# Moving weight splits behind later ScalarE copies, and alternating accumulator banks, in a block-matrix up-projection

## The chip, the cores and the metric

The kernel runs on one core of one Trainium2 chip. The metric is device time in microseconds (us); a run's time is that of its one core. The kernel before was timed three times: 1277.96, 1278.49 and 1284.9 us, median 1278.49.

## What is computed

A two-layer decoder trunk on 512 tokens of width 1024, float32. Each layer has a sequence mixer (mLSTM and forgetting attention in layer 0, Mamba-2 and pooling in layer 1), a layer norm, a gated convolutional FFN and a second layer norm:

```
def conv_ffn(x, w_up, conv_w, conv_b, w_down):
    h = causal_dwconv(x @ w_up, conv_w, conv_b)      # width 3 along the sequence
    val, gate = jnp.split(h, 2, axis=-1)
    return (jax.nn.silu(gate) * val) @ w_down        # D_FF = 2816

x = layer_norm(ALPHA * x + y, ln1_g[layer], ln1_b[layer])
f = conv_ffn(x, ffn_w_up[layer], ffn_conv_w[layer], ffn_conv_b[layer], ffn_w_down[layer])
x = layer_norm(ALPHA * x + f, ln2_g[layer], ln2_b[layer])
```

The change touches only `x @ w_up`, once per layer.

## The kernel before

Every float32 operand is cut into two parts, hi and lo, and a matrix product is three products of parts: hi by hi, lo by hi, hi by lo. The cut of a weight tile (`split`, L284) is a copy to hi on ScalarE (ACT, L285), then a subtraction that gives lo on VectorE (DVE, L286). Five hi and five lo buffers serve all weight tiles.

**Direct tiles.** The up-projection has 22 gate tiles and 22 value tiles, each 128 features wide. A pair (one gate, one value) can be computed directly: `mtile` loads a weight tile, splits it and issues 24 matmuls of 512 columns (L238). `gated` (L996) then does the convolution: per tile an ACT activation (L990) and two DVE operations (L992), then a Silu (L998) and a DVE product (L1000).

**Rounds.** Eight of the 22 pairs are computed directly. The other fourteen are taken two pairs at a time in `up_quarters` (L1022): seven rounds per layer (j = 3, 6, ..., 21), each with a Strassen-Winograd scheme on 2 by 2 blocks, which needs seven block products in place of eight. A round has four weight blocks W11, W12, W21, W22 (512 KB each). Sums of weight blocks are made by DMA: a transfer issued on GpSimd (POOL) that adds a block from HBM onto a tile already in SBUF. Sums of the activations (E, S2, S3, S4) are made once per layer, in round 1. In the order of the code, a round does:

- load W11 into c and W12 into d (L1087, L1089; four buffers, so that loads run up to two rounds ahead), W21 and W22 into two "raw" buffers (L1090, L1091). The loads are issued on SP.
- L1092: d += W22. This is called d's sum below.
- Product 1: split c, x = c times A11; ACT copies it to g (L1099).
- L1100: c += W12, the first sum.
- Product 2: split W21, o = W21 times A12; DVE adds it to g (L1105).
- Product 3: split c, y = c times E; ACT copies it to v (L1110).
- L1111: c += W22, the second sum.
- The direct pair j + 1 (two tiles), except in round 7.
- Product 4: split c, x += c times S2; ACT copies to v (L1117).
- L1118: c += W21, the third sum.
- Product 5: split d, x += d times S3; DVE (L1122). Product 6: split W22, y += W22 times S4; DVE (L1126).
- Product 7: split c, x += c times A22; ACT copies to g (L1130), first for pair half i = 0, then for i = 1; then `gated` of both pairs.

Each product is done for the two halves i = 0 and 1, each 12 matmuls of 256 columns (L1069). The two halves' x tiles accumulate through the round in two banks of PSUM with the tag "S" (L1095), of which there are two in all; "tp" and "av" are two further banks, used elsewhere in the kernel for transposes and the output projections. The remaining four banks ("mm") hold o, y and the direct tiles. So the x of a round takes the banks that the x of the round before held until its L1130 copies.

**Order.** The program is written in the order above, but a scheduler at compile time orders each engine's instructions by when, by its own estimate of times, their inputs are ready. An instruction may stand on its engine ahead of ones that come earlier in the code. The emitted order is fixed; at run time each engine takes its instructions one after another, and an instruction that waits holds up those behind it. `tc.issue_after(ins)` adds an edge for the scheduler: instructions traced in its block that run on the engine of `ins` are placed behind `ins`; it puts no wait into the program.

Of the kernel before, what the change touches and what calls it, by code (L numbers as in the profile page):

```python
# [16 lines left out]
NJ = DFF // P  # L17
# [89 lines left out]
def trunk(ctx: ExitStack, tc: tile.TileContext, W, x, xT, cols, rows, poolw, consts, out):  # L107
# [15 lines left out]
    def nm(s):  # L123
        uid[0] += 1
        return f"{s}_{uid[0]}"

    def ps(tag="mm"):
        return pp.tile([P, 512], F32, tag=tag, name=nm(tag), bufs={"mm": 4, "S": 2, "tp": 1, "av": 1}[tag])
# [39 lines left out]
    def c1(i):  # L168
        return col[:, i:i + 1]
# [114 lines left out]
    def split(src, hi, lo, lo_eng=None):  # L284
        A.activation(hi, src, AF.Copy)  # L285
        (lo_eng or V).tensor_tensor(lo, src, r32(hi), ALU.subtract)  # L286
# [696 lines left out]

    def ffn(pool, layer, up, dn, last):
        cw, cb = C_FW[layer], C_FB[layer]
        act = [pool.tile([P, 2, S], F32, tag="a", name=nm("a"), bufs=NJ // 2) for _ in range(NJ // 2)]

        def conv(j, o):
            c = tmp()
            A.activation(c, o, AF.Identity, bias=c1(cb + j), scale=c1(cw + 2 * 2 * NJ + j))  # L990
            for d in range(1, 3):
                V.scalar_tensor_tensor(c[:, d:], o[:, :S - d], c1(cw + (2 - d) * 2 * NJ + j), c[:, d:],  # L992
                                       ALU.mult, ALU.add)
            return c

        def gated(j, g, v):  # L996
            gt = conv(NJ + j, g())
            A.activation(gt, gt, AF.Silu)  # L998
            vl = conv(j, v())
            V.tensor_tensor(act[j // 2][:, j % 2, :], vl, gt, ALU.mult)  # L1000

        with tc.tile_pool(name=f"up{layer}", bufs=1, side="left") as work:
            up_quarters(work, up, gated)
        after_ln[:] = [None, 0]
        for t in range(NT):
            xk[t] = rp.tile([P, D], F32, tag="x", name=nm("xk"), bufs=4)
            nc.sync.dma_start(xk[t], away[t])
        with tc.tile_pool(name=f"dn{layer}", bufs=1, side="left") as work:
            early = [0, 1]

            def two(b):
                if early:
                    early.pop()
                    hi, lo = (wp.tile([P, D], F32R, tag=g, name=nm("s"), bufs=5).rearrange("p (a b) -> p a b", a=2)
                              for g in ("hi", "lo"))
                else:
                    hi, lo = (work.tile([P, 2, S], F32R, tag="s", name=nm("s"), bufs=11) for _ in range(2))
                split(act[b], hi, lo, G)
                return [(hi[:, i, :], lo[:, i, :]) for i in range(2)]
            proj_ln(two, range(NJ), dn, 2 * layer + 1, None if last else OD)  # L1020

    def up_quarters(pool, up, gated):  # L1022

        L, R = slice(0, 256), slice(256, 512)

        def quarter(h, t):
            return [xcur[2 * part + h][:, :, t] for part in range(2)]

        A11, A12, A21, A22 = quarter(0, L), quarter(1, L), quarter(0, R), quarter(1, R)

        def wide(tag, dt=F32):
            return pool.tile([P, 4, 256], dt, tag=tag, name=nm(tag), bufs=1)

        def pair():
            return [pool.tile([P, 4, 256], F32R, tag="o", name=nm("o"), bufs=6) for _ in range(2)]

        def total(eng, d, terms):

            eng.tensor_tensor(d, r32(terms[0][1][0]), r32(terms[1][1][0]), ALU.add if terms[1][0] > 0 else ALU.subtract)  # L1041
            for sign, a in ((terms[0][0], terms[0][1][1]), (terms[1][0], terms[1][1][1])):
                eng.tensor_tensor(d, d, r32(a), ALU.add if sign > 0 else ALU.subtract)  # L1043

        def more(eng, d, s, a, op):
            eng.tensor_tensor(d, s, r32(a[0]), op)
            eng.tensor_tensor(d, d, r32(a[1]), op)

        gated(0, lambda: mtile(up), lambda: mtile(up + 1))
        e, s2 = wide("e"), wide("t")  # L1050
        total(V, e, [(1, A22), (-1, A21)])
        E, S2, S3 = pair(), pair(), pair()
        split(e, *E)
        more(V, s2, e, A11, ALU.add)
        A.activation(S2[0], s2, AF.Copy, scale=-1.0)
        V.scalar_tensor_tensor(S2[1], s2, -1.0, r32(S2[0]), ALU.mult, ALU.subtract)
        gated(1, lambda: mtile(up + 2), lambda: mtile(up + 3))

        def wsplit(p):
            hi = wp.tile([P, D], F32R, tag="hi", name=nm("hi"), bufs=5)  # L1060
            lo = wp.tile([P, D], F32R, tag="lo", name=nm("lo"), bufs=5)
            split(p, hi, lo)
            return hi, lo

        def mul(o, w, half, a, start=True):
            n = 0
            for ww, part in ((w[0], 0), (w[1], 0), (w[0], 1)):
                for k in range(4):
                    T.matmul(o[:, L], ww[:, half * 512 + k * P:half * 512 + (k + 1) * P], a[part][:, k, :],  # L1069
                             start=start and n == 0, stop=n == 11, skip_group_check=not start)  # L1070
                    n += 1

        for j in range(3, NJ, 3):
            js = (j - 1, j)
            W11, W12, W21, W22 = (W[up + 2 * (j - 1) + i] for i in range(4))
            if j == 3:
                for i in range(4):
                    sl = slice(i, i + 1)
                    total(G, e[:, sl], [(1, [a[:, sl] for a in A11]), (-1, [a[:, sl] for a in A21])])
                    split(e[:, sl], *(a[:, sl] for a in S3))  # L1080
                S4 = wide("e", F32R), wide("f", F32R)
                for i in range(4):
                    sl = slice(i, i + 1)
                    more(G, s2[:, sl], s2[:, sl], [a[:, sl] for a in A12], ALU.subtract)
                    split(s2[:, sl], *(a[:, sl] for a in S4))
            c, d = (rp.tile([P, D], F32, tag="x", name=nm("c"), bufs=4) for _ in range(2))
            nc.sync.dma_start(c, W11)  # L1087
            e21, e22 = wraw(), wraw()
            nc.sync.dma_start(d, W12)  # L1089
            nc.sync.dma_start(e21, W21)  # L1090
            nc.sync.dma_start(e22, W22)  # L1091
            nc.gpsimd.dma_start(d, W22, accum_op=ALU.add)  # L1092
            g = [pool.tile([P, S], F32, tag="g", name=nm("g"), bufs=2) for _ in js]
            v = [pool.tile([P, S], F32, tag="v", name=nm("v"), bufs=2) for _ in js]
            x = [ps("S") for _ in js]  # L1095
            w = wsplit(c)
            for i in range(2):
                mul(x[i], w, i, A11)
                A.activation(g[i][:, L], x[i][:, L], AF.Copy)  # L1099
            nc.gpsimd.dma_start(c, W12, accum_op=ALU.add)  # L1100
            w = wsplit(e21)
            for i in range(2):
                o = ps()
                mul(o, w, i, A12)
                V.tensor_tensor(g[i][:, L], g[i][:, L], o[:, L], ALU.add)  # L1105
            w = wsplit(c)
            y = [ps() for _ in js]
            for i in range(2):
                mul(y[i], w, i, E)
                A.activation(v[i][:, R], y[i][:, L], AF.Copy, scale=-1.0)  # L1110
            nc.gpsimd.dma_start(c, W22, accum_op=ALU.add)  # L1111
            if j + 1 < NJ:
                gated(j + 1, lambda: mtile(up + 2 * j + 2), lambda: mtile(up + 2 * j + 3))
            w = wsplit(c)
            for i in range(2):
                mul(x[i], w, i, S2, False)
                A.activation(v[i][:, L], x[i][:, L], AF.Copy)  # L1117
            nc.gpsimd.dma_start(c, W21, accum_op=ALU.add)  # L1118
            w = wsplit(d)
            for i in range(2):  # L1120
                mul(x[i], w, i, S3, False)
                V.tensor_tensor(v[i][:, R], v[i][:, R], x[i][:, L], ALU.subtract)  # L1122
            w = wsplit(e22)
            for i in range(2):
                mul(y[i], w, i, S4, False)
                V.scalar_tensor_tensor(v[i][:, L], v[i][:, L], -1.0, y[i][:, L], ALU.mult, ALU.subtract)  # L1126
            w = wsplit(c)
            for i in range(2):
                mul(x[i], w, i, A22, False)
                A.activation(g[i][:, R], x[i][:, L], AF.Copy)  # L1130
                gated(js[i], lambda: g[i], lambda: v[i])

    with tc.tile_pool(name="ev", bufs=1, side="left") as pool:
# [120 lines left out]
```

## Time and profile before

| | |
|---|---|
| times of three runs | 1277.96, 1278.49, 1284.9 us |
| the profiled execution: time, span | 1282.55 us, 1280.5 us |
| TensorE matmul (PE) busy | 1169.7 us, 91% |
| VectorE (DVE) busy | 838.7 us, 65% |
| ScalarE (ACT) busy | 563.0 us, 44% |
| GpSimd (POOL) busy | 335.0 us, 26% |
| TensorE's mean granted clock, share of full | 0.955 |

The span runs from the first to the last instruction of the profiled execution; some 2 us lie around it. The rounds of layer 0 lie between about 266 and 557 us of the span, those of layer 1 between about 856 and 1145 us. The busy share of PE counts a matmul at half clock as busy for twice as long.

### The profile page before, as it was taken

How to read it: one execution, taken by the hardware profiler on the slowest of the kernel's cores; microseconds unless marked ns; L12 is line 12 of the kernel's file. 1: busy time of each engine (PE TensorE's matmuls, PEld its weight loads, DVE VectorE, ACT ScalarE, POOL GpSimd, SP SyncE). 2: the span in 40 equal slices, each digit the busy share in tenths (PEclk: the TensorE clock that was granted, in tenths of full speed). 3: DMA queues.
4: the chain of work that ended last, by engine and by line, in shares of the span. 5: the costliest groups of instructions: out<-in, count | busy, mean ns of one | idle time of the engine just before them, and what ended most of it. 6: DMA issues, size and time to landing. Idle time of an engine off the chain costs nothing. (4 is left out here: it accounts for less than half of the span.)

```text
span 1280.5 us, 16455 instructions
## 1 busy us (share of the span) xinstructions
PE 1169.7 (91%) x6320; PEld 1000.5 (78%) x6320; DVE 838.7 (65%) x1254; ACT 563.0 (44%) x889; POOL 335.0 (26%) x330
## 2 busy tenths in 40 slices
PE   8999999997789888989999999998888888998997
PEld 6777788876789778978887766777777778987886
DVE  5978555696556656674548978687665655675545
ACT  5446533134444544463324466324354543455330
POOL 1223222125010001047422066025100101027442
PEclk9999999998899888989999999998888889999998
DMA  8322421264656465463323142345545465544211
GB/s 289 110 98 88 159 84 66 99 201 102 141 134 159 119 148 118 115 194 100 99 66 119 51 137 98 116 137 138 139 129 148 110 154 132 149 115 158 93 46 66
DMA packets 47950, 157.70 MB, mean 123 GB/s; under 512 B 5352, under 2 KB 5992, under 8 KB 47872
## 3 DMA queue, kind: packets, MB, share of 16 engines
q1 hardware_dynamic: 39648, 126.77, 29.6%
q0 software_dynamic: 8224, 29.89, 13.4%
q8 instruction: 49, 0.80, 0.2%
q14 instruction: 29, 0.24, 0.1%
HBM read 150.30 MB, written 6.34 MB: 122 GB/s over the span
## 5 line engine op out<-in xcount | busy, mean ns | idle before, releaser
L286 DVE TENSOR_TENSOR lo<-raw,hi 128x1024 fp32r<-128x1024 f32 (+1 forms) x173 | 239.6, 1390 | 128.1 <-ACT hi L285 127.5
L238 PE MATMUL mm<-xT,hi 128*128 128x512 f32 (+1 forms) x1088 | 281.6, 400 | 2.0 <-ACT xT L285 2.0
L285 ACT ACTIVATE hi<-raw 128x1024 fp32r<-128x1024 f32 (+1 forms) x175 | 172.2, 989 | 168.2 <-PE mm L336 102.4
L238 PEld LDWEIGHTS mm<-xT,hi 128*128 128x128 f32 x1088 | 202.4, 191 | 45.6 <-issue 4.4
L286 DVE TENSOR_TENSOR lo<-c,hi 128x1024 fp32r<-128x1024 f32 x70 | 84.3, 1220 | 123.1 <-ACT hi L285 123.1
L285 ACT ACTIVATE hi<-c 128x1024 fp32r<-128x1024 f32 x70 | 73.7, 1056 | 183.6 <-DMA c<-in_W 175.1
L286 POOL TENSOR_TENSOR s<-a,s 128x1024 fp32r<-128x1024 f32 x44 | 119.0, 2719 | 108.0 <-PE mm L336 54.5
L238 PE MATMUL mm<-xT,lo 128*128 128x512 f32 (+1 forms) x544 | 139.8, 393 | 0.0
L1069 PE MATMUL S<-xT,hi 128*128 128x256 f32 x448 | 85.1, 333 | 57.2 <-ACT g L1130 52.3
L336 PE MATMUL mm<-hi,s 128*128 128x512 f32 (+1 forms) x396 | 120.9, 385 | 6.6 <-POOL s L286 5.9
L1069 PEld LDWEIGHTS S<-xT,hi 128*128 128x128 f32 x448 | 75.3, 240 | 60.1 <-ACT g L1130 54.4
L238 PEld LDWEIGHTS mm<-xT,lo 128*128 128x128 f32 x544 | 101.7, 190 | 21.7 <-issue 1.9
L336 PEld LDWEIGHTS mm<-hi,s 128*128 128x128 f32 x396 | 74.9, 192 | 21.9 <-POOL s L286 6.9
L992 DVE SCALAR_TENSOR_TENSOR tmp<-mm,col,tmp 128x511 f32<-128x511 f32 (+1 forms) x64 | 47.3, 747 | 51.0 <-ACT tmp L990 50.0
L336 PE MATMUL mm<-lo,s 128*128 128x512 f32 (+1 forms) x198 | 75.8, 383 | 0.0
L1069 PE MATMUL S<-o,hi 128*128 128x256 f32 x448 | 65.3, 283 | 1.2 <-ACT v L1117 1.2
L1069 PEld LDWEIGHTS S<-o,hi 128*128 128x128 f32 x448 | 59.5, 191 | 2.3 <-ACT v L1117 1.4
L336 PE MATMUL S<-hi,s 128*128 128x512 f32 x176 | 56.9, 390 | 0.0
L990 ACT ACTIVATE tmp<-mm,col 128x512 f32<-128x512 f32 x32 | 24.6, 776 | 67.7 <-PE mm L238 58.8
L314 POOL TENSOR_SCALAR small<-small 128x1 f32<-128x1 f32 (+2 forms) x25 | 13.7, 548 | 154.8 <-DVE small L413 93.4
L1069 PE MATMUL mm<-o,hi 128*128 128x256 f32 x224 | 36.0, 294 | 17.2 <-DVE tmp L992 14.6
L1092 POOL DMA_DIRECT2D c<-in_W x14 | 12.3, 880 | 150.2 <-DMA c<-in_W 62.6
(286 smaller groups left out, 2241.8 us busy)
## 6 DMA issues: line engine op xcount, KB each, us to landing
raw<-in_W SPq DMA_DIRECT2D x162, 512.0 KB, 3.7
c<-in_W POOLq DMA_DIRECT2D x56, 512.0 KB, 7.1
c<-in_W SPq DMA_DIRECT2D x28, 512.0 KB, 3.9
bc<-dr SPq DMA_DIRECT2D x20, 256.0 KB, 4.1
tmp<-in_rows SPq DMA_DIRECT2D x16, 256.0 KB, 3.9
away<-xk SPq DMA_DIRECT2D x8, 512.0 KB, 2.6
xk<-away SPq DMA_DIRECT2D x8, 512.0 KB, 6.7
raw<-in_W SPq DMA_DIRECT2D x8, 256.0 KB, 5.7
```

The source lines that it names most:

```text
L238: T.matmul(o[:, :cols_], w[:, k * P:(k + 1) * P], xs_(xcur, part, k)[:, :cols_], start=n == 0, stop=n == 3 * NK - 1)
L285: A.activation(hi, src, AF.Copy)
L286: (lo_eng or V).tensor_tensor(lo, src, r32(hi), ALU.subtract)
L314: G.tensor_scalar(dst, var, EPS, None, ALU.add)
L336: T.matmul(o[:, c], a[:, t * P:(t + 1) * P], ww[:, kk * 512 + c.start:kk * 512 + c.stop], start=first and kk == 0 and n == 0, stop=fin and ...
L990: A.activation(c, o, AF.Identity, bias=c1(cb + j), scale=c1(cw + 2 * 2 * NJ + j))
L992: V.scalar_tensor_tensor(c[:, d:], o[:, :S - d], c1(cw + (2 - d) * 2 * NJ + j), c[:, d:], ALU.mult, ALU.add)
L1069: T.matmul(o[:, L], ww[:, half * 512 + k * P:half * 512 + (k + 1) * P], a[part][:, k, :], start=start and n == 0, stop=n == 11, skip_group ...
L1092: nc.gpsimd.dma_start(d, W22, accum_op=ALU.add)
```

## The change

Three edits, all in the rounds.

1. **Order on ACT.** `wsplit` gets a second argument. The hi copy of the first sum (product 3) is placed behind the L1130 copy of half i = 0 of the round before (`box["quarter"]`; in round 1 behind the last L1099 copy of the same round). The hi copy of the second sum (product 4) is placed behind the last L1110 copy of product 3. The hi copy of the third sum (product 7) is placed behind the convolution's first activation (L990) of the value tile of the direct pair; in round 7, which has none, behind the last L1110 copy. The subtractions on DVE get no edge.
2. **Banks.** The x tiles of a round use "tp" and "av" in odd rounds and the two "S" banks in even ones.
3. **d's sum** is written after the first sum in the code, behind product 1's copies, and no longer right behind the loads.

```diff
     def ffn(pool, layer, up, dn, last):
+        box = {}
         def conv(j, o):
             c = tmp()
-            A.activation(c, o, AF.Identity, bias=c1(cb + j), scale=c1(cw + 2 * 2 * NJ + j))
+            box["conv"] = A.activation(c, o, AF.Identity, bias=c1(cb + j), scale=c1(cw + 2 * 2 * NJ + j)).ins
...
-        def wsplit(p):
+        def wsplit(p, after=None):
             hi = wp.tile([P, D], F32R, tag="hi", name=nm("hi"), bufs=5)
             lo = wp.tile([P, D], F32R, tag="lo", name=nm("lo"), bufs=5)
-            split(p, hi, lo)
+            if after is None:
+                split(p, hi, lo)
+            else:
+                with tc.issue_after(after):
+                    split(p, hi, lo)
             return hi, lo
...
-            nc.gpsimd.dma_start(d, W22, accum_op=ALU.add)
-            x = [ps("S") for _ in js]
+            x = [ps(b) for b in (("S", "S"), ("tp", "av"))[j // 3 % 2]]
             w = wsplit(c)
             for i in range(2):
                 mul(x[i], w, i, A11)
-                A.activation(g[i][:, L], x[i][:, L], AF.Copy)
+                got = A.activation(g[i][:, L], x[i][:, L], AF.Copy).ins
             nc.gpsimd.dma_start(c, W12, accum_op=ALU.add)
+            nc.gpsimd.dma_start(d, W22, accum_op=ALU.add)
...
-            w = wsplit(c)
+            w = wsplit(c, box.get("quarter", got))
             y = [ps() for _ in js]
             for i in range(2):
                 mul(y[i], w, i, E)
-                A.activation(v[i][:, R], y[i][:, L], AF.Copy, scale=-1.0)
+                got = A.activation(v[i][:, R], y[i][:, L], AF.Copy, scale=-1.0).ins
             nc.gpsimd.dma_start(c, W22, accum_op=ALU.add)
             if j + 1 < NJ:
                 gated(j + 1, lambda: mtile(up + 2 * j + 2), lambda: mtile(up + 2 * j + 3))
-            w = wsplit(c)
+                mid = box["conv"]
+            else:
+                mid = got
+            w = wsplit(c, got)
...
-            w = wsplit(c)
+            w = wsplit(c, mid)
             for i in range(2):
                 mul(x[i], w, i, A22, False)
-                A.activation(g[i][:, R], x[i][:, L], AF.Copy)
+                got = A.activation(g[i][:, R], x[i][:, L], AF.Copy).ins
+                if i == 0:
+                    box["quarter"] = got
                 gated(js[i], lambda: g[i], lambda: v[i])
```

## Rows read from the trace of the kernel before

**Rows 1.** Waits: engine, tile, line, releaser: us in total, times, longest.
```profile
PE S L1069 <- ACT g L1130: 52.3, 10, 6.2
```

**Rows 2.** The chain that ended last, 915 to 1000 us: start, us, what.
```profile
916.10 1.24 DVE lo L286
917.35 3.62 DMA c<-in_W
...
921.55 0.52 POOL c L1092
922.07 9.18 DMA c<-in_W
...
933.66 5.49 PE S L1069 x24
```

**Rows 3.** Timeline of PE, 340 to 420 us: start, us, instruction, [idle before].
```profile
371.55 0.64 PE L1069 MATMUL mm<-e,hi 128*128 128x256 f32 x4
...
376.83 0.64 PE L1069 MATMUL S<-xT,hi 128*128 128x256 f32 x4
381.77 1.22 PE L1069 MATMUL S<-xT,hi 128*128 128x256 f32 x4 [4.30 <-ACT g L1130]
```

**Rows 4.** Timeline of ACT, 340 to 420 us.
```profile
363.51 1.06 ACT L285 ACTIVATE hi<-c 128x1024 fp32r<-128x1024 f32 x1 [2.17 <-DMA c<-in_W]
...
366.00 0.78 ACT L990 ACTIVATE tmp<-mm,col 128x512 f32<-128x512 f32 x1 [0.91 <-PE mm L238]
366.68 1.05 ACT L285 ACTIVATE hi<-c 128x1024 fp32r<-128x1024 f32 x1
...
369.15 1.05 ACT L285 ACTIVATE hi<-raw 128x1024 fp32r<-128x1024 f32 x1
379.45 1.06 ACT L285 ACTIVATE hi<-c 128x1024 fp32r<-128x1024 f32 x1 [9.24 <-DMA c<-in_W]
```

**Rows 5.** Windows over product 1 of ten rounds: us, PE, PEld busy, PEclk, DMA, GB/s.
```profile
381.77:387.00 5.23, 5.23 (x26) 5.23 (x26) 0.53 0.68 116
...
sum 51.54, PE 51.52 PEld 51.53; mean PE 5.15 PEld 5.15
```

**Rows 6.** The chain that ended last, into round 7 of layer 1.
```profile
1115.47 2.88 PE mm L1069 x24
1118.35 5.76 PE S L1069 x48
```

**Rows 7.** Issue to landing of L1100, then of L1118: us min/median/max.
```profile
DMA to landing us min/median/max: 5.1/9.2/11.1
...
DMA to landing us min/median/max: 7.1/7.4/8.5
```

**Rows 8.** Timelines of POOL and ACT into round 7 of layer 0.
```profile
523.71 0.86 POOL L1100 DMA_DIRECT2D c<-in_W  x1 [12.81 <-DVE lo L286]
...
529.10 1.06 ACT L285 ACTIVATE hi<-c 128x1024 fp32r<-128x1024 f32 x1 [4.97 <-DMA c<-in_W]
```

**Rows 9.** Timeline of DVE, 340 to 420 us.
```profile
380.53 1.22 DVE L286 TENSOR_TENSOR lo<-c,hi 128x1024 fp32r<-128x1024 f32 x1 [6.92 <-ACT hi L285]
...
390.96 1.22 DVE L286 TENSOR_TENSOR lo<-raw,hi 128x1024 fp32r<-128x1024 f32 x1
```

**Rows 10.** Round 1: timelines of PE and ACT, layer 1, then layer 0.
```profile
901.61 1.20 PE L1069 MATMUL mm<-o,hi 128*128 128x256 f32 x4 [8.81 <-DVE tmp L992]
...
900.54 0.36 ACT L1099 ACTIVATE g<-S 128x256 f32<-128x256 f32 x1
...
309.89 0.55 PE L1069 MATMUL mm<-o,hi 128*128 128x256 f32 x1 [5.80 <-DVE tmp L992]
...
294.94 1.06 ACT L285 ACTIVATE hi<-c 128x1024 fp32r<-128x1024 f32 x1 [9.49 <-DMA c<-in_W]
```

**Rows 11.** Round 7 of layer 0: timeline of ACT.
```profile
536.94 2.01 ACT L285 ACTIVATE hi<-c 128x1024 fp32r<-128x1024 f32 x2 [2.27 <-DMA c<-in_W]
...
540.59 0.65 ACT L1110 ACTIVATE v<-mm 128x256 f32<-128x256 f32 x2
```

More of the change, by code (lines that the diff above doesn't have):

```diff
@@ L1002, in ffn @@
         with tc.tile_pool(name=f"up{layer}", bufs=1, side="left") as work:
-            up_quarters(work, up, gated)
+            up_quarters(work, up, gated, box)
         after_ln[:] = [None, 0]
@@ L1020, in ffn, with up_quarters @@
             proj_ln(two, range(NJ), dn, 2 * layer + 1, None if last else OD)
-    def up_quarters(pool, up, gated):
+    def up_quarters(pool, up, gated, box):
         L, R = slice(0, 256), slice(256, 512)
```

## The prediction, made before the changed kernel ran

> **What bounds the kernel now.** I read the page first: PE is busy 91% of the span, every other engine much less, so time is won only where PE waits or runs at a lower clock. The view of waits names the largest wait of PE that repeats: ten times, 52.3 us in total, the first matmul of a round waits for an L1130 copy [rows 1]. Ten is five a layer, the starts of rounds 2 to 6. The timelines show one of them, from round 2 to round 3. PE ends product 7 at 376.83 + 0.64 = 377.47 us and stands 4.30 us [rows 3]. ACT meanwhile stands 9.24 us before the hi copy of the next round's first sum, which the scheduler put ahead of the L1130 copies; it starts when the DMA lands, at 379.45 [rows 4]. So x's bank comes free late because ACT waits for a sum that PE needs only two products later.
>
> The chain of waits says why the sum is late: the third sum's lo, then d's load (3.62 us), d's sum issued on POOL, and the first sum behind it, 9.18 us, with the bank wait at its end [rows 2]. Here d is that of two rounds on, c that of the next.
>
> The wait costs twice. Product 1 after it takes 5.23 us at a granted clock of 0.53, near the lower of the two levels, 1.2 of 2.4 GHz, after 4.30 us without a matmul; ten of them take 51.54 us [rows 5]. A product at full clock takes 2.88 us [rows 6]. Round 7 starts without a gap, products 7 and 1 together in 5.76 us [rows 6]: that is what a round's start is without this wait.
>
> **The change, part by part.** The sum is made against the profiled execution, 1282.55 us with a span of 1280.5; that is 4.06 us above the median of the runs, 1278.49, and I carry the difference over to the median.
>
> *Banks (edit 2).* The x of a round takes banks that the round before doesn't use, so product 1 no longer waits for L1130. The wait goes: -52.3 us [rows 1]. With PE fed, product 1 stays at the upper clock: ten times 5.15 - 2.88 = 2.27 us, -22.7 us [rows 5, 6]. Together -75.0 us. What is late next? Not product 1's operands: W11's hi copy runs at 366.68, ten microseconds ahead [rows 4]. Next is what DVE and ACT must do before the following products, which is the next term.
>
> *First sum behind L1130 of half 0 (edits 1 and 3).* The hi copy now stands behind one L1130 copy but still ahead of the other and of the two pairs' convolutions. When does the sum land? The third sum's hi copy, now at 363.51, must go behind the L990 of 366.00 [rows 4]. That takes ACT's place after 366.68, so W11's hi copy moves on by up to 1.06 us, and the sum's issue to about 371.2. d's load follows the third sum's lo (about 369) and takes 3.62 us [rows 2], so d's sum is ready near 372.6 and should be issued after the first sum, whichever stands first in the code. Free of d's sum, the first sum took 529.10 - 523.71 = 5.4 us in round 7 [rows 8]; behind it the median is 9.2 [rows 7]. I take 7.4 us, the third sum's median [rows 7], since the new place has two ordinary loads beside it as the third sum has. So it lands at 378.6, 1.1 us after product 7's end.
>
> From there DVE decides. Between lo of the first sum (380.53) and the end of lo of the first direct tile (392.18) lie 11.65 us [rows 9], nearly all packed DVE work (convolutions, products). Some 2.1 of it (a lo, an L1126, short waits for PE) can now run before, which leaves 9.5. So that lo is ready at 378.6 + 1.1 + 9.5 = 389.2; PE wants it after products 1 to 3 and eight hi matmuls of 512 columns (a matmul of 256 columns is 2.88 / 24 = 0.12 us, so these are 1.9), at 377.47 + 3 x 2.88 + 1.9 = 388.0. Stall 1.2 us, ten times: +12. Ends: none if the sum lands after 5.4 us, 3.0 each (+30) if after 9.2.
>
> *Third sum behind the direct tile (edit 1).* Its split now falls into the stretch in which W22 for product 6 is split. That hi copy runs at 369.15 and its product starts at 371.55 [rows 3, 4]; pushed by 1.06 us to end at 371.3, its lo (1.2 us) would be ready at 372.5, 0.5 us after the four hi matmuls are through. By priority in the code the scheduler may keep it in place. I take 0.3 us in twelve rounds (1 to 6, two layers): +3.6, between 0 and 12.7. The second sum's hi, behind L1110, is not used before the direct tiles are done (48 matmuls of 512 columns, some 11 us at 0.24 each); they hide it.
>
> *Round 7 (edit 1).* Here no direct tiles stand between, and the chain of sums is PE's limit. The second sum's hi copy ran at 536.94, ahead of L1110 at 540.59 [rows 11]; now it comes behind it, at 540.59 + 0.65 = 541.2 at the latest, 4.3 us later. But product 4 can't start before product 3 is done, which is about when L1110 runs, so most of the 4.3 us was spent waiting anyway, and PE loses only what of hi and lo the old order had already done by then. I take 0.7 us. Twice: +1.4, between 0 and 2 x 4.3.
>
> *Round 1 (edit 1).* The first sum waits behind the last L1099. In layer 1 that copy runs at 900.54, while product 3's first half was already done; its second half stood until 901.61 for a convolution on DVE [rows 10]. The first half now joins it: +1.44 us. In layer 0 the hi copy blocked ACT for 9.49 us, and the same product waited 5.80 us [rows 10]; ACT gets that time back, but DVE's queue still leads there. I take 1.44 twice, +2.9; ends -5.8 and +2 x 2.9.
>
> Sum: -75.0 + 12 + 3.6 + 1.4 + 2.9 = -55.1. The profiled execution would take 1227.4, the median run **1223 us**.
>
> ScalarE's order deserves a second look, since the wait is moved and not removed. The row shows an ACT that stands 9.24 us before one copy while L1130's matmuls had ended [rows 4]. The Trainium skill (PSUM — Partial Sum Buffer, section Engine vs sequencer instructions) says that the queues of ScalarE, VectorE and GpSimd are strictly first in, first out; the trace agrees. By that rule the waiting copy, one place further on, still holds the second L1130 copy and both convolutions, which is the second rival below; free of it, the sum would stand at -67.1 rather than -55.1.
>
> The row on landing is 7.4 us for the third sum against 5.4 for the unaccompanied first [rows 7, 8]. The Trainium skill (DMA: Bandwidth & Descriptors, section Issuing engines are not separate DMA queues) says that transfers from all issuing engines run on the same 16 engines and interleave, so taking d's sum from in front leaves the loads on SP beside it. With 5.4 the sum would be -67, with 7.4 it is -55.
>
> **The rivals.**
>
> *A: the first sum still lands late.* If W11's lo slips, or the scheduler keeps d's sum in front with its data there in time, the landing is 9.2 us after an issue at 371.2, at 380.4, and the stall 3.0 us each; with the other added terms at twice my value the gain is 75.0 - 30 - 16 = 29. For it: POOL takes requests in order and the edit leaves each round's d far ahead. Against: d's load now ends later. Time 1250, within 1233 to 1263.
>
> *B, the other side: d's sum stays ahead and waits for its load.* POOL then stands until d's load lands, 369 + 3.62 = 372.6; the first sum is issued at 373.2 and lands 9.2 later at 382.4, 4.9 us after product 7. ACT can't do L1130 of half 1 or the convolutions before; the direct tile's lo comes at 393.0, 5.0 us late, and product 1's low clock is paid there instead (2.3 us, rows 5). That is 7.3 of the 7.5 us that a round start gives back; with the other terms at their upper middle (+16) the time is 1278.5 - 2 + 16 = 1292. It decides when the sum lands more than about 4 us after product 7. For it: the chain of waits runs through just these steps today [rows 2]. Against: by the scheduler's own clock the first sum should be ready first.
>
> *C: the scheduler arranges it otherwise*, so that the banks are free and another wait of the same length (a direct tile's weight, a weight buffer) takes its place: within 6 us of 1278.
>
> **How the numbers follow.** Forecast 0.68, A 0.17, C 0.07, B 0.08. The forecast's own range is 1204 (all terms but -75 at nothing) to 1238. For 8 in 10 I reach into A: **1204 to 1254**. What this kernel's timing can tell from no change is about 0.5%, 6.4 us. Faster: forecast and A and a little of C, 0.87; same: most of C, 0.05; slower: B, 0.08.
>
> **What would show it.** Right: no wait for L1130 at PE; product 1 of rounds 2 to 6 at 2.9 us and a clock of 1.0; rounds 2 to 6 of 31 to 33 us each (7 x 2.88 for products and 11 for the direct pair is 31.1); the first sum issued before d's and landing within 8 us. Wrong on the third term: PE stalls of over 2 us before the first direct tile, with lo on DVE as releaser. Wrong on round 1 or 7: product 3 of round 1 or product 4 of round 7 over 3 us later than said. The prediction as a whole is wrong if a gap of over 3 us still recurs in rounds 2 to 6.

## The result, and the profile after

The changed kernel takes 1207.3 us (median of four runs, one of them disturbed, at 2359 us, and left out of the ratio) against 1280.5 for the kernel before on the same chip: a ratio of 0.9411, 95% interval 0.9363 to 0.9459. The prediction said 1223 with a range of 1204 to 1254. The profiled execution took 1201.96 us, 80.6 less than that of before. Line numbers below are those of the changed kernel: product matmuls L1075, the copies L1104, L1116, L1126 and L1139 (before: L1099, L1110, L1117, L1130), first sum L1105, d's sum L1106, second sum L1117, third sum L1127; each experiment shifts them by a line or a few.

The page: span, busy shares, granted clock in 40 slices.

```profile
span 1199.5 us, 16425 instructions
PE 1141.1 (95%) x6320; PEld 973.1 (81%) x6320; DVE 832.0 (69%) x1254; ACT 562.9 (47%) x889; POOL 339.2 (28%) x330
PEclk9999999999899999999999999999899999999999
```

The waits of PE, to be held against [rows 1]: no wait for L1139 is left. The largest is one in round 1 of each layer.

```profile
PE mm L1075 <- ACT hi L285: 19.0, 2, 10.2
PE mm L336 <- POOL s L286: 7.6, 4, 3.2
PE S L261 <- ACT xT L285: 5.3, 2, 4.2
```

The timeline of PE over the start of round 3, to be held against [rows 3]: product 7 ends and product 1 follows without a gap, now in "tp" and "av".

```profile
365.52 0.64 PE L1075 MATMUL S<-xT,hi 128*128 128x256 f32 x4
366.00 0.64 PE L1075 MATMUL tp<-xT,hi 128*128 128x256 f32 x4
```

The windows over product 1 of rounds 2 to 6 in both layers, to be held against [rows 5] (columns also DVE, ACT and POOL busy): ten times 2.88 us at a granted clock of 1.00, which is 2.4 GHz, where it was 5.15 us at about half of that.

```profile
366.00:368.88 2.88, 2.88 (x26) 2.88 (x25) 2.20 (x3) 2.88 (x5) 0.68 (x1) 1.00 1.04 208
...
sum 28.80, PE 28.80 PEld 28.80 DVE 22.01 ACT 28.38 POOL 6.81; mean PE 2.88 PEld 2.88 DVE 2.20 ACT 2.84 POOL 0.68
```

From product 1 of round 2 to that of round 7 in layer 0 it is 334.94 to 491.66 us, 31.3 a round; before it was 343.88 to 531.25, 37.5.

Timelines of ACT and of POOL at the same place, to be held against [rows 4] and the POOL steps of [rows 2]: ACT takes the first L1139 copy before the first sum's hi copy and stands only 0.44 us before that; POOL issues the first sum ahead of d's sum.

```profile
364.76 0.38 ACT L1139 ACTIVATE g<-S 128x256 f32<-128x256 f32 x1 [5.87 <-PE S L1075]
365.59 1.06 ACT L285 ACTIVATE hi<-c 128x1024 fp32r<-128x1024 f32 x1 [0.44 <-DMA c<-in_W]
...
367.97 0.36 ACT L1139 ACTIVATE g<-S 128x256 f32<-128x256 f32 x1
```

```profile
360.20 0.87 POOL L1105 DMA_DIRECT2D c<-in_W  x1 [11.85 <-DVE lo L286]
362.14 0.87 POOL L1106 DMA_DIRECT2D c<-in_W  x1 [1.07 <-DMA c<-in_W]
```

The landing of the first sum, then of d's sum (issue to landing, us), to be held against [rows 7]: 5.3 in place of 9.2 for the first sum.

```profile
DMA to landing us min/median/max: 5.0/5.3/9.4
```

```profile
DMA to landing us min/median/max: 5.8/7.7/8.9
```

Why did POOL's order turn? In the kernel before, two inputs were ready almost together. The rows of SP and POOL there: d's load is issued once the third sum's lo has freed its buffer, at 365.86; d's sum follows at 369.87, and the first sum, whose own input was ready with a lo that ended at 369.49, right behind it at 370.41.

```profile
365.86 0.33 SPq L1089 DMA_DIRECT2D c<-in_W  x1
```

```profile
369.87 0.87 POOL L1092 DMA_DIRECT2D c<-in_W  x1 [12.90 <-DVE lo L286]
370.41 1.22 POOL L1100 DMA_DIRECT2D c<-in_W  x1
```

With the third sum's split behind the direct tile's activation, d's load starts later against the rest of the round, and the scheduler puts the first sum ahead. That this is its reason is inferred; the runs below show that POOL's order turns wherever this edge stands, and without it stays as before unless an edge on GpSimd itself turns it. By an estimate from these rows the order itself is worth 4.8 us: 0.9 at the issue (370.41 - 369.49) and 3.9 at the landing (9.2 - 5.3). The whole change doesn't get all of it, since the same edge also puts W11's hi copy, and with it the issue of the first sum, behind one more copy on ACT. Held against the end of product 7, the sum landed 2.0 us late before (379.45 against 377.47) and lands 0.6 us early now (365.59 against 366.16).

### The profile page after: what moved, and what is told of

It is laid out like the page before. It is cut to its first block, busy times and chain, and to the rows that moved or that the text cites. A ratio compares the mean times of both kernels' runs of the same rounds, so it can differ in the third digit from the quotient of the medians.

```text
span 1199.5 us, 16425 instructions
## 1 busy us (share of the span) xinstructions
PE 1141.1 (95%) x6320; PEld 973.1 (81%) x6320; DVE 832.0 (69%) x1254; ACT 562.9 (47%) x889; POOL 339.2 (28%) x330
## 4 chain that ended last, share of the span: by engine, by line
PE 68%; DVE 10%; DMA 9%; issue 5%; POOL 4%; ACT 3%; SPq 0%; POOLq 0%; DVEq 0%; ACTq 0%
PE mm L238 21%; PE mm L336 13%; DMA c<-in_W 8%; PE S L336 7%; PE mm L1075 6%; PE tp L336 3%; DVE lo L286 3%; PE S L1075 3%; PE av L336 3%; PE tp L1075 2%; PE av L1075 2%; ACT hi L285 2%; DVE tmp L993 1%; PE mm L278 1%; PE S L261 1%
## 5 line engine op out<-in xcount | busy, mean ns | idle before, releaser
L1105 POOL DMA_DIRECT2D c<-in_W x14 | 12.5, 895 | 150.0 <-DVE lo L286 140.6
L1075 PE MATMUL mm<-o,hi 128*128 128x256 f32 x224 | 36.2, 297 | 19.0 <-ACT hi L285 19.0
L1127 POOL DMA_DIRECT2D c<-in_W x14 | 12.1, 865 | 128.3 <-DVE lo L286 121.4
L1075 PEld LDWEIGHTS mm<-o,hi 128*128 128x128 f32 x224 | 32.1, 206 | 19.4 <-ACT hi L285 19.4
L993 DVE SCALAR_TENSOR_TENSOR tmp<-g,col,tmp 128x511 f32<-128x511 f32 (+1 forms) x56 | 45.3, 808 | 0.0
L285 ACT ACTIVATE s<-a 128x1024 fp32r<-128x1024 f32 x44 | 45.1, 1043 | 0.0
```

## The experiments

Three theories were set against each other in the first four. B: the alternating banks take the wait away, as the prediction's sum has it. Q: the order on GpSimd does, which the third sum's edge turns. A: the first sum's edge on ScalarE does. In the later expectations A, R and T name the rival of that run alone. All ratios are to the kernel before on the same chip, with 95% intervals.

**Banks alone** (edit 2 without the edges on ScalarE and without edit 3).

```diff
-            x = [ps("S") for _ in js]
+            x = [ps(b) for b in (("S", "S"), ("tp", "av"))[j // 3 % 2]]
```

> Edit 2 alone: x alternates between two pairs of banks; order and sums as before. Three theories of where the gain of the change (about 73 us) comes from. Theory Q (queue): from the third sum's edge, which delays d's load and so puts the first sum in front of d's sum on GpSimd; then the sum lands before product 7 ends and nothing has to wait. Theory B (banks): from the x banks alone, since PE waited for them. Theory A (ScalarE): from moving the first sum's hi copy behind the L1130 copy. B expects 1205 to 1212 us here. Q expects the wait to move: the first sum still lands about 9 us after its issue, ScalarE still stands before its hi copy, and behind it stands the hi copy of W21, so PE waits at product 2 instead, about 2.8 us at each of ten round starts, the clock staying up: 1225 to 1245 us. A expects no more than half of the gain: over 1240.

Measured: 1277.9 us, ratio 0.9973 (0.9959 to 0.9988). B fell. The wait for the copies of L1130 is gone, but the first direct tile now waits for its own bank, which DVE frees (product 2's addition, here L1111) behind the first sum's lo. The largest wait of PE:

```profile
PE mm L238 <- DVE g L1111: 38.5, 10, 4.4
```

POOL at the start of round 3, in the order of before (L1098 is d's sum, L1106 the first sum):

```profile
370.19 0.87 POOL L1098 DMA_DIRECT2D c<-in_W  x1 [12.60 <-DVE a L1001]
370.72 1.22 POOL L1106 DMA_DIRECT2D c<-in_W  x1
```

And the landing of the first sum:

```profile
DMA to landing us min/median/max: 5.5/9.1/10.7
```

The sum still lands after 9.1 us, ACT stands 10.16 us before its hi, and what stands behind that hi is late whichever bank it frees. A's bound, over 1240, holds. Q had the wait moving, but named product 2 as the new place, one step too early, and its 1225 to 1245 is far too low: it took the clock to stay up. PE is busy for 1174.2 us here, against 1169.7 before and 1141.1 in the whole change, so the time at the lower clock is still paid, now behind the wait at the direct tile, whose first eight matmuls take 3.78 us in most rounds and 2.00 in the changed kernel.

**The edges on ScalarE alone** (edit 1: all three, banks as before).

```diff
-            w = wsplit(c)
+            w = wsplit(c, box.get("quarter", got))
...
-            w = wsplit(c)
+            w = wsplit(c, got)
...
-            w = wsplit(c)
+            w = wsplit(c, mid)
```

> Edit 1 alone: the three edges on ScalarE; x stays in the two S banks. Q expects nearly the whole gain: the first sum in front on GpSimd lands in 5 to 6 us; product 1's first half starts without a wait, its second half waits for the second L1130 copy, which stands behind the first sum's hi copy, about 0.9 us at ten starts: 1210 to 1222 us. A expects the same. B expects the bank wait to stay at over 3 us each: 1245 or more.

Measured: 1219.1 us, ratio 0.9513 (0.948 to 0.9546), as Q and A had it; B fell again. The first sum lands after 5.5 us (median), and of the bank wait a fifth is left:

```profile
PE S L1075 <- ACT g L1139: 10.1, 12, 1.7
```

**The third sum's edge alone.**

```diff
-            w = wsplit(c)
+            w = wsplit(c, mid)
```

> Only the third sum's edge of edit 1: neither the other two edges nor the banks nor the moved d's sum. The first sum's hi copy stays ahead of both L1130 copies. Q expects that this alone gives most of the gain, since the first sum now stands before d's sum on GpSimd and lands, as it did in round 7 of the kernel before, by the time that product 7's first half is done: 1205 to 1222 us, first sum's landing near 5.4 us. A and B expect the waits for L1130 to stay: 1260 or more.

Measured: 1242.8 us, ratio 0.9694 (0.9666 to 0.9723). Faster than A and B allowed, 21 us slower than Q's range. The edge, which sits at another product, turns POOL's order and the first sum lands after 5.6 us (median); but its hi stands ahead of the L1139 copy on ACT, and nearly half of the wait stays (23.1 of 52.3 us). The issue of the first sum on POOL, then ACT, then PE:

```profile
364.65 0.86 POOL L1106 DMA_DIRECT2D c<-in_W  x1 [12.63 <-DVE lo L286]
```

```profile
370.38 1.06 ACT L285 ACTIVATE hi<-c 128x1024 fp32r<-128x1024 f32 x1 [7.04 <-DMA c<-in_W]
371.34 1.04 ACT L285 ACTIVATE hi<-raw 128x1024 fp32r<-128x1024 f32 x1
372.29 0.36 ACT L1139 ACTIVATE g<-S 128x256 f32<-128x256 f32 x1
```

```profile
372.70 1.22 PE L1075 MATMUL S<-xT,hi 128*128 128x256 f32 x4 [2.10 <-ACT g L1139]
```

The sum was issued at 364.65, 5.95 us before product 7's end (372.70 - 2.10). It needed 5.7 to land (until 370.38), 1.9 for the two hi copies and 0.4 for the L1139 copy: 8.0, which is 2.0 too many; PE waited 2.10.

**The whole change without the third sum's edge.**

```diff
-            w = wsplit(c, mid)
+            w = wsplit(c)
```

> The whole change without the third sum's edge: its hi copy goes back to where the scheduler put it, d's load starts early again and d's sum stands in front of the first sum on GpSimd. Q expects the first sum to land about 9 us after its issue, ScalarE to wait for it behind the first L1130 copy, and PE to wait about 3 us at each of ten round starts (for the direct tile's lo on DVE, or for product 3's weights): 1225 to 1245 us. A and B expect the time of the changed kernel, 1203 to 1212.

Measured: 1268.0 us, ratio 0.9891 (0.9851 to 0.9932). Without that one edge 61 of the 73 us are gone again. A and B, which expected the changed kernel's time, fell; Q's range had the direction and was 23 us too low. POOL's order is back (L1106 is d's sum, which stands until its load lands), the first sum lands after 9.2 us (median), and the wait is the one that the banks alone showed, ten times 2.8 us. What Q left out is the clock again: PE is busy for 1168.1 us, 27 more than in the whole change, and the eight matmuls behind this wait take 3.48 us where the changed kernel has 2.00. POOL, then PE:

```profile
366.91 0.87 POOL L1106 DMA_DIRECT2D c<-in_W  x1 [13.30 <-DMA c<-in_W]
367.44 1.22 POOL L1105 DMA_DIRECT2D c<-in_W  x1
```

```profile
384.52 3.48 PE L238 MATMUL mm<-xT,hi 128*128 128x512 f32 x8 [2.92 <-DVE g L1111]
```

**GpSimd's order alone.** If this is the cause, one edge on GpSimd must do it, with neither banks nor edges on ScalarE.

```diff
-            nc.gpsimd.dma_start(d, W22, accum_op=ALU.add)
...
-            nc.gpsimd.dma_start(c, W12, accum_op=ALU.add)
+            one = nc.gpsimd.dma_start(c, W12, accum_op=ALU.add).ins
+            with tc.issue_after(one):
+                nc.gpsimd.dma_start(d, W22, accum_op=ALU.add)
```

> The kernel before with one edge alone: d's sum is placed behind the first sum of its own round on GpSimd; no edge on ScalarE, banks as before. Theory Q (the first sum was late because it stood behind d's sum, which waits for d's load on GpSimd): the first sum lands after 5 to 6 us (median) instead of 9.2, the time is like that of the third sum's edge alone, 1225 to 1245. Rival R (the third sum's edge won its time by the place of its own split on ScalarE, not by the order on GpSimd): 1265 to 1281, and the waits of ScalarE for the first sum stay above 80 us.

Measured: 1209.3 us, ratio 0.945 (0.9412 to 0.9488), overlapping the whole change's. R fell, and Q's own range was 16 us too high, since it took the third sum's edge for the measure of the order's worth. That edge delays W11's split and so the issue of the first sum; without it the sum is issued at 358.50, some 7.6 us before product 7's end, and ACT is through with its hi just in time, though it takes its copies in the old order. POOL at the start of round 3 (L1107 is d's sum):

```profile
358.50 0.87 POOL L1105 DMA_DIRECT2D c<-in_W  x1 [11.86 <-DVE lo L286]
359.04 1.24 POOL L1107 DMA_DIRECT2D c<-in_W  x1
```

The landing of the first sum, then of d's sum: the two have traded places, and the one issued 0.5 us behind the other takes some 9 us, whichever it is.

```profile
DMA to landing us min/median/max: 5.0/5.3/7.0
```

```profile
DMA to landing us min/median/max: 8.9/9.1/11.2
```

ACT at the same place (L1140 is the copy that frees the bank), and what is left of the bank wait:

```profile
363.85 1.06 ACT L285 ACTIVATE hi<-c 128x1024 fp32r<-128x1024 f32 x1 [5.06 <-DMA c<-in_W]
364.82 1.04 ACT L285 ACTIVATE hi<-raw 128x1024 fp32r<-128x1024 f32 x1
365.76 0.36 ACT L1140 ACTIVATE g<-S 128x256 f32<-128x256 f32 x1
```

```profile
PE S L1075 <- ACT g L1140: 1.6, 5, 0.4
```

ACT still waits 5.06 us for the sum here, and that costs next to nothing, because L1140 then runs about when PE needs the bank: the ten starts of a round that cost 52.3 us cost 1.6 now.

**The whole change without the first sum's edge.**

```diff
-            w = wsplit(c, box.get("quarter", got))
+            w = wsplit(c)
```

> The whole change without the first sum's edge on ScalarE (its hi copy may stand ahead of the last copies of the round before again). With the third sum's edge alone TensorE waited 23.1 us for these copies and one product in two rounds ran at the lower clock; alternating banks take that wait away. Theory Q with banks that pay once the first sum lands early: 1215 to 1232, no wait of TensorE for L1139 in rounds 2 to 6. Rival A (the wait moves in full to the first direct tile's bank, which VectorE and ScalarE free behind the same hi copy): 1238 to 1248, and that wait appears at L238.

Measured: 1207.1 us, ratio 0.942 (0.9385 to 0.9455). A fell, and Q was 8 us too high: next to the banks and the third sum's edge, the first sum's edge, which is the one that the change's words put first, is worth nothing that can be measured. The banks are worth something here: the third sum's edge alone took 1242.8 us, and with the banks, the second sum's edge and edit 3 beside it this kernel takes 36 us less. The third sum's edge brings the first sum about 2 us too late for the old banks, as the run with that edge alone showed, and the other banks cover just that; the first sum's edge covers most of it too, since all three edges without the banks took 1219.1.

**The whole change, GpSimd's order in place of the third sum's edge.**

```diff
-            w = wsplit(c, mid)
+            w = wsplit(c)
...
-            nc.gpsimd.dma_start(c, W12, accum_op=ALU.add)
-            nc.gpsimd.dma_start(d, W22, accum_op=ALU.add)
+            one = nc.gpsimd.dma_start(c, W12, accum_op=ALU.add).ins
+            with tc.issue_after(one):
+                nc.gpsimd.dma_start(d, W22, accum_op=ALU.add)
```

> The whole change without the third sum's edge (that kernel took 1267.98), with one edge on GpSimd in its place: d's sum behind the first sum of its round. Theory Q (the third sum's edge was worth only the order that it brings about on GpSimd): 1200 to 1212, the first sum lands after at most 6 us (median). Rival T (the place of the third sum's split on ScalarE matters by itself): 1225 to 1250.

Measured: 1217.5 us, ratio 0.9498 (0.9473 to 0.9524). Of the 60.7 us that the edge's removal had cost, the order on GpSimd gives back 50.4; the rest, about 10, was foreseen by neither theory. The profile shows part of it: product 5 waits for L1127, ACT's copy of product 4, behind the third sum's hi, 5.8 us in seven waits (these rows); the profiled run itself took 1211.0. So beside the other two edges and the banks the third sum's edge has a small worth apart from the order; GpSimd's order alone doesn't need it.

```profile
PE tp L1075 <- ACT v L1127: 3.0, 4, 1.5
PE S L1075 <- ACT v L1127: 2.8, 3, 1.2
```

**Banks and GpSimd's order, no edge on ScalarE.** The diffs are those of the first experiment and of GpSimd's order.

> The kernel before with d's sum behind the first sum on GpSimd and with alternating banks; no edge on ScalarE. If banks and ScalarE's edges have nothing left to remove once the first sum lands early: within 0.5% of 1209.3 (GpSimd's order alone) and of 1207.3 (the whole change), 1203 to 1213. If ScalarE's edges carry weight of their own in the whole change: over 1215. If banks carry weight of their own: under 1203.

Measured: 1213.6 us, ratio 0.9483 (0.9457 to 0.951), 0.6 us above the first case's range and below the second's. The interval overlaps that of GpSimd's order alone: no gain from the banks on top of it shows. Here product 5 waits for L1127 for 14.7 us in total. Whether it is really a little slower than the order alone these runs don't tell.

**Round 1.** The two waits left (19.0 us) stand in round 1 of each layer. The timeline of ACT in layer 0: product 1's copies and the first sum's hi stand behind the splits of S4 (e<-t), which wait for sums on POOL (L1048).

```profile
304.95 0.42 ACT L285 ACTIVATE e<-t 128x256 fp32r<-128x256 f32 x1 [2.00 <-POOL t L1048]
306.08 0.42 ACT L285 ACTIVATE e<-t 128x256 fp32r<-128x256 f32 x1 [0.71 <-POOL t L1048]
306.40 0.37 ACT L1104 ACTIVATE g<-tp 128x256 f32<-128x256 f32 x1
306.66 0.38 ACT L1104 ACTIVATE g<-av 128x256 f32<-128x256 f32 x1
306.93 1.06 ACT L285 ACTIVATE hi<-c 128x1024 fp32r<-128x1024 f32 x1
```

So the block that makes S3 and S4 was moved behind product 3, and in a second kernel S4's sums also to DVE.

```diff
+            if j == 3:
+                for i in range(4):
+                    total(G, e[:, sl], ...)
+                    with tc.issue_after(got):
+                        split(e[:, sl], *(a[:, sl] for a in S3))
...
-                    more(G, s2[:, sl], s2[:, sl], ...)
+                    more(V, s2[:, sl], s2[:, sl], ...)
+                    with tc.issue_after(got):
+                        split(s2[:, sl], *(a[:, sl] for a in S4))
```

> The whole change, and in round 1 the sums S3 and S4 on GpSimd and their splits are moved behind product 3 (ScalarE's splits of them behind its copies). Theory: the 9 to 10 us that TensorE still stands in round 1 of each layer come from these splits, which stand ahead of product 1's copies on ScalarE and wait for GpSimd: 1184 to 1195, and the wait goes. Rival: GpSimd's S4 then ends after product 6 wants it (or the wait only changes its place): 1200 to 1210.

> As the kernel with late splits, with S4's two sums on VectorE in place of GpSimd (eight quarter tiles each). If GpSimd's sums end too late there, this is faster than it by 3 to 8 us; if VectorE's queue in round 1 is the limit, slower by 2 to 10 us than it.

Measured: 1205.9 us, ratio 0.9417 (0.9391 to 0.9444), for the block on POOL: the 19.0 us wait goes, but products 4 and 5 of the round wait in its place, and the rival holds. With S4 on DVE 1197.4 us, ratio 0.9344 (0.9305 to 0.9383): 8.5 us less, a little more than expected. The largest wait of round 1 left in layer 0 is at product 5 (in layer 1 it is 3.4 us, for a lo on DVE):

```profile
321.01 1.23 PE L1075 MATMUL tp<-o,hi 128*128 128x256 f32 x4 [4.06 <-ACT v L1128]
```

**Put together.** The same step on top of banks and GpSimd's order, and on top of the whole change with GpSimd's order.

> As the one with banks and GpSimd's order, with round 1's S3 and S4 behind product 3 and S4's sums on VectorE (a step that took the whole change from 1207.3 to 1197.4). If round 1's stall is independent of ScalarE's edges: 1193 to 1203. If what it won came with the first sum's edge in round 1: 1204 to 1212.

> The whole change with GpSimd's order and round 1's late S3 and S4. GpSimd issues here as in the late kernel with VectorE's sums but with no wait of a sum for another load: 1190 to 1199, the same as that kernel (1197.4) if nothing on GpSimd is left to win; slower than it by over 0.5% only if d's sum, now beside the following sum, is late for product 5.

Measured: 1202.2 us, ratio 0.938 (0.9355 to 0.9405), inside its first case, and 1199.1 us, ratio 0.9353 (0.9331 to 0.9375), at the upper end of its range. So round 1's step takes 11.4 us off the kernel without edges on ScalarE, as off the changed one (9.9): it doesn't need them. The best two kernels, 1197.4 and 1199.1, can't be told apart; both medians lie 8 to 10 us below the changed kernel, but their intervals still touch its own, so that they beat it is likely and not proved.

Edit 3 was not run by itself: with it or without it, the scheduler emits the same order on all five engines.

## Why the prediction was right, and where it was not

*Bank wait, -52.3.* It went, as said, and rounds 2 to 6 take 31.3 us, within the 31 to 33 named. But the term was credited to the banks. By themselves these gave 3 us; GpSimd's order gave 71 by itself, with the banks as before. The prediction had the chain right (d's load, d's sum, first sum, ACT, bank) and saw that d's sum would fall behind, but it used that only to size a stall of ScalarE and DVE. That the same shift takes the wait away at its root, it didn't see. So the range was hit in part by luck: with the banks and the other edges but the old order on GpSimd the time is 1268, outside it.

*Cold product 1, -22.7.* 51.5 us became 28.8: right to the tenth.

*First sum and DVE, +12.* This is the step that failed in size: the sum was put at 7.4 us from issue to landing, with 1.2 us of stall ten times; it landed in 5.3, and there is no such stall. The lower end that the prediction gave for 5.4 us, nothing, was the answer. The row on the unaccompanied sum [rows 8] was nearer than the third sum's. For the first sum and d's, a landing of 5.3 stands for the one at the head of GpSimd's queue and 9 for the one right behind it. Not for every sum: the third, issued some 10 us after the sum before it, takes 7.4 us before [rows 7] and 7.2 after:

```profile
378.76 0.87 POOL L1127 DMA_DIRECT2D c<-in_W  x1 [9.69 <-DVE lo L286]
```

```profile
DMA to landing us min/median/max: 5.6/7.2/9.0
```

So the guess that the first sum would behave like the third, for the loads on SP beside both, was wrong, and what makes the third slower stays open. The Trainium skill (DMA: Bandwidth & Descriptors, section Issuing engines are not separate DMA queues) says that transfers of all issuing engines interleave on the same 16 engines; the 7.4 was read from the third sum's row, not from that rule, and the measurement decides against that reading, not against the rule.

*Third sum, +3.6.* The waits of PE for L1126, the copy beside it on ACT, come to 0.9 us in all. Too much by some 3 us, inside its bounds of 0 to 12.7. What the edge brought on GpSimd, 61 us by the run without it, was outside of any bound given to this term.

*Round 7, +1.4.* The sign was wrong. From product 1 to the first matmul of the down-projection it takes 22.3 us in layer 0 (25.8 before) and 22.4 in layer 1 (23.8 before). Each round 7 had two waits before, 6.9 us in all; now there is one of 1.47 us each.

*Round 1, +2.9.* The wait is 10.2 and 8.8 us (8.4 and 8.8 before). From product 1 of the round to the end of its product 7 it takes 67.7 us in layer 0 (71.0 before, without the bank wait behind it) and 69.7 in layer 1 (71.7 before): a gain of 5.3 where a cost stood, just inside the bound of -5.8.

*Rival A* (the sum still lands late) and *rival B* (d's sum stays ahead) didn't come about, but the whole change without the third sum's edge shows parts of both. As in A, the sum lands after 9.2 us and PE stalls 2.8 us on average before the direct tile, where the prediction had put 3.0; as in B, d's sum stands for its load and the lower clock is paid behind that stall. A, at 1250, had left the clock out; measured are 1268. The Trainium skill's rule that ScalarE's and VectorE's queues are first in, first out (PSUM — Partial Sum Buffer, section Engine vs sequencer instructions) was weighed as a danger, and the banks alone show it at work: the same late hi copy holds up ScalarE (10.16 us), then DVE, then the next bank (38.5 us of PE's time in all).

Part by part, the terms with rows are the bank wait (-52.3), product 1 (-22.7), round 1 (-5.3) and round 7 (-4.9), -85.2 together. Measured from product 1 of round 1 to the down-projection, the two layers gain 84.4 us, and the rest of the kernel, which the change doesn't touch, took 3.4 more in this execution. Against the profiled execution the forecast of 1227.4 is 25.4 too high: about 12 for the first sum, 8 for round 1, 6 for round 7 and 3 for the third sum, less those 3.4.

## What to carry to other kernels

When an engine stands before an instruction that waits for a transfer, follow the transfer back to the queue that issues it, and ask what stands in front of it there; one edge in that queue gave 71 us where three edges and other banks together gave 73. More buffers behind a late producer can move the wait to the next thing that it frees (52.3 us at one bank became 38.5 at another, 3 us won); they helped where the producer was late by only some 2 us. The test for such a wait is the lead: from the issue of the transfer to the moment when the consumer's engine is needed for something else, against landing plus the work queued behind it (5.95 against 8.0 us cost 2 us a round; 7.6 against about 7.6 cost 0.4 at most).

## What the runs showed of the hardware

Of two sums by DMA of 512 KB, issued 0.5 us apart on GpSimd, the second takes 9.0 to 9.2 us from issue to landing (medians). The first sum, with none close before it, takes 5.3 to 5.6; but that alone doesn't settle it, since the third sum, also with none close before it, takes 7.2 to 7.4. Loads of the same size into c and d on SP took 3.9 us before and 3.6 after (medians), though over product 1 the DMA engines' busy share rose from 0.68 to 1.04 and the rate from 116 to 208 GB/s. The length of PE's idle time alone didn't tell what clock follows: behind 4.30 us [rows 3] and behind 2.10 us (the third sum's edge alone) four matmuls of 256 columns took 1.22 us, near the lower level, while behind 2.75 us elsewhere in that same run they took 0.74, and with the banks alone eight of 512 columns took 2.12 us behind 3.65 us and 3.78 behind 3.50. The mean granted clock also differs from run to run, and the span with it: three runs of the changed kernel show 0.986, 0.982 and 0.977 for spans of 1199.5, 1203.5 and 1205.0 us.
